# A two-layer decoder trunk in split float32: row sums sent behind the blocks' reads, squares added before their sums, one weight chunk in other buffers

## The chip, the cores and the metric

The kernel runs on one core of a Trainium2 chip. The metric is device time in microseconds of one execution, median of the runs. PE is TensorE (matmuls; PEld its weight loads), DVE is VectorE, ACT ScalarE, POOL GpSimd, SP SyncE, which here issues nearly all DMAs. Each engine works through its own queue in order and waits for the others on semaphores.

## What is computed

512 tokens and 16 meta tokens (T = 528) of width 1024 pass two layers. Each layer is an RMS norm, one wide input projection, two parallel mixers (causal pooling in four groups, and latent attention with 8 heads), gates, an up-projection each and an output projection on the residual:

```python
for l in range(DEPTH):
    h = rmsnorm(h_res, norm_gain[l])
    proj = h @ w_in[l]
    u_pool, z_pool, c_q, c_kv, k_rope, z_mla, g_pool, g_mla = jnp.split(proj, IN_SPLIT_POINTS, axis=-1)
    y_pool = (pool_mix(u_pool, pool_w_group[l], pool_scale[l]) * jax.nn.silu(z_pool)) @ pool_w_up[l]
    o_mla = mla(c_q, c_kv, k_rope, pos, q_a_norm_gain[l], kv_a_norm_gain[l], w_q_b[l], w_kv_b[l],
                q_norm_gain[l], k_norm_gain[l])
    y_mla = (o_mla * jax.nn.silu(z_mla)) @ mla_w_up[l]
    merged = jax.nn.sigmoid(g_pool) * y_pool + jax.nn.sigmoid(g_mla) * y_mla
    h_res = h_res + merged @ w_out[l]
```

Inside `mla` the compressed queries (768 wide) and keys (256 wide) are normed, expanded to 8 heads of 64 plain and 32 rotary dimensions, normed again per head over those 96 dimensions (query and key), rotated and used in causal softmax attention. The result is float32.

## The kernel before

**Tiles.** All activations lie transposed: 128 channels on partitions, up to 528 tokens along the free dimension, worked in halves of 264 (`FULL`) or, in the last layer, in one stretch of 512. Every large matmul is done as three (`mm3`, L204 on): weights and activations are each split in a high and a low part, and hi x hi, hi x lo and lo x hi are summed in PSUM (L205 to L207). Weights come in chunks of 128 x 512: `fetch` issues the load into one of three `raw` buffers, ACT makes `whi` (L200), DVE `wlo` (L201). Three buffers each hold these; a chunk marked `spare` goes to a wide buffer (`th`) instead, of which there are two and which the attention also uses.

**Order.** `stream` is one generator of all large matmuls in a fixed order: the compressed keys and queries (ckv, cq), pooling inputs (u), keys (k), values (v), gates of the pool (zp), pooling (y), queries (qr, qn), the up-projection of the pool (pu), the rest of the gates (zm, gp, gm), the attention's up-projection (mu0 to mu7), the output projection (o). `Layer.go` runs the special work and advances the stream between its steps: `up(name)` until a projection is done, `fill_now(ns)` and `fill` for so many planned nanoseconds of matmuls, `after(ns, fn)` puts a function that far on. A scheduler then fixes each engine's order. `behind(a, b)` makes a wait for b, `follow(a, b)` keeps only the order.

**Norm sums.** The squares of the tokens (layer 1: `square_x`, in tiles `cq` and `q`; layer 0 sums the tokens by rows on ACT) and of the two halves of the compressed keys (`csq`, L485) are summed over channels by a matmul with a block of ones (L426): each uses 32 columns, so that four stand side by side in the array, at positions 0, 32, 64 and 96, two token halves times two inputs. POOL adds the token squares in pairs and pairs of pairs first (L382), which leaves two tiles. The rotary key follows at once in matmuls of the same form (`kr_sums`, L501). The sums go to DRAM and back, spread over 16 partitions (`nq`), are turned into inverse roots by DVE in small steps (`newton`), and are read back for all partitions.

**Statistics.** For the norms per head, squares of keys, rotary keys, queries (four tiles qn, 64 plain dimensions of two heads each) and rotary queries (two tiles qr, 32 dimensions of four heads each) are summed by matmuls of 16 columns with blocks of ones as weights (`stat_go`, L535), again at four positions: two token halves, two in turn. `q_stat` makes the squares of the queries on ACT (L730).

**Attention.** For each head `prep` copies the head's keys and queries together (POOL, L807 to L811), `head` computes scores for blocks of 128 queries, their exponentials (ACT, L840, into `pa`, `cq8`, `cq10`) and row sums (`rs`), and transposes the blocks into `attD` (DVE, L846). The blocks go to DRAM (`pdr`, L906) and come back in another order in four reads of `attE` (L915); ACT and DVE split them (`parts`, L958, L959), and `pv` multiplies with the values (L980, L983) two heads later. The row sums go to DRAM (`rdr`, L907) and come back spread over 64 partitions (L920, a `cq` tile); for every second head, POOL multiplies the gate with them (L924). POOL also saves 16 columns of each block (L843) from the buffers of the exponentials. The reads are put `BACK` (7800) planned nanoseconds on, the gate `LATE` (13000).

```python
            via = pdr[h % 2]
            sp.dma_start(via, blocks)
            sp.dma_start(row.rearrange("a (p i) -> p (a i)", i=4), rs[:, 0:4])
```

Of the kernel before, what the change touches and what calls it, by code (L numbers as in the profile page):

```python
# [19 lines left out]
DEPTH = 2  # L20
D = 1024
# [9 lines left out]
NEG = -1e30  # L31
TWO_PI = 2.0 * math.pi
SWAP = [i ^ 16 for i in range(32)]
MAGIC = float(1.5 * 2.0 ** 23)
# [46 lines left out]
def trunk(ctx, tc, xT, xrow, mrow, pos, win, wkr, wqb, wkb, wvb, wgr, wpu, wmu, wout, gains, const, yT):  # L81
# [255 lines left out]
    scr = dp.tile([P, 8, SEQ], F32, name="scr")  # L337
    nsr = [dp.tile([4, T], F32, name=f"nsr{l}") for l in range(DEPTH)]
    ndr = [dp.tile([3, T], F32, name=f"ndr{l}") for l in range(DEPTH)]
# [8 lines left out]
    class Layer:  # L348
        def __init__(self, l):
            self.l, self.last = l, l == DEPTH - 1  # L350
            self.XS = XTOK if self.last else FULL
            self.x0 = NM if self.last else 0
            self.xt = xt if l == 0 else [None] * 8
            self.hs, self.us, self.zps = hbuf, [None] * 4, [None] * 4
            self.cs, self.cqs, self.ys, self.am = [None] * 2, [None] * 6, [None] * 4, [None] * 8
            self.kn, self.qn, self.zms, self.ogs = [None] * 4, [None] * 4, [None] * 4, [None] * 4
            self.qr, self.qf = [None] * 2, [None] * 2
            self.gms, self.mg, self.xr, self.vw = [None] * 8, [None] * 8, [None] * 8, []
            self.made = [None] * 8
            self.csq, self.xsq = [None] * 2, [None] * 8  # L360
            self.sq, self.half = [], halves()
            self.hosted = self.st = self.acc = self.inv = self.cinv = self.kraw = self.kp = None
# [13 lines left out]
        def square_x(self, k):  # L376
            self.xsq[k] = slot(f"cq{4 + k}" if k < 4 else f"q{k}")
            made = act.activation(self.xsq[k][:, :T], self.xt[k][:, :T], AF.Square)
            for w in (1, 2):
                if k % (2 * w) == 2 * w - 1:  # L380
# [26 lines left out]
        def norm_sums(self):  # L407
            if self.l:
                fill_now(2600)
            else:  # L410
# [11 lines left out]
            for k in range(0, len(runs), 2):  # L422
                for s, (a, b) in enumerate(FULL):
                    for ps, t, m, start, stop in runs[k:k + 2]:
                        g = 64 * s + 32 * (m % 2)
                        mm = pe.matmul(ps[g:g + 32, :HALF], ones[:, 0:32], t[:, a:b], start=start, stop=stop,  # L426
                                       tile_position=(0, g))
                        if t is not self.csq[1]:
                            behind(mm, self.csq_last)
            self.kr_sums()  # L430
            sums = tmp()
            for s, (a, b) in enumerate(FULL):
                if self.l:
                    act.activation(sums[0:64, a:b], px[64 * s:64 * s + 64, :HALF], AF.Copy)
                dve.tensor_copy(sums[64:128, a:b], pc[64 * s:64 * s + 64, :HALF])
            raw, norms = nsr[self.l], ndr[self.l]
            if self.l:
                sp.dma_start(raw, sums[0:97:32, 0:T])
            else:
                sp.dma_start(raw[2:4], sums[64:97:32, 0:T])  # L440
# [5 lines left out]
            nq = sm.tile([16, 4, C], F32, tag="nq", name=nm("nq"))  # L446
# [3 lines left out]
            dve.scalar_tensor_tensor(out=na[:, 0, :], in0=nq[:, 1, :], scalar=1.0 / D, in1=na[:, 0, :],  # L450
                                     op0=ALU.mult, op1=ALU.add)
            dve.tensor_scalar(na[:, 1, :], na[:, 0, :], EPS, None, op0=ALU.mult)
            dve.tensor_scalar(ny[:, 2, :], na[:, 1, :], EPS, None, op0=ALU.mult)
            for m in range(2):
                dve.scalar_tensor_tensor(out=na[:, 1, :], in0=nq[:, 2 + m, :], scalar=1.0 / 256,
                                         in1=na[:, 1, :], op0=ALU.mult, op1=ALU.add)
            newton(ny[:, 0:2, :], na, nt)
# [266 lines left out]

        def q_stat(self, ps, a, b, c):
            for a0, b0 in FULL:
                a0, b0 = max(a, a0), min(b, b0)
                if a0 < b0:
                    q = next(self.half)
                    made = act.activation(q[:, :b0 - a0], ps[:, a0 - a:b0 - a], AF.Square)  # L730
                    self.stat(q[:, :b0 - a0], a0, b0, c, made)

        def ev_qr(self, r):
            def ev(ps, a, b):
# [4 lines left out]
                act.activation(f[:, a:b], ps, AF.Copy, scale=self.g(G_QR))  # L739
                self.q_stat(ps, a, b, C_IR + 4 - 4 * r)  # L740

# [4 lines left out]
        def ev_qn(self, p):  # L746
            def ev(ps, a, b):
                if a == self.x0:
                    self.qn[p] = slot(f"q{p}")
                act.activation(self.qn[p][:, a:b], ps, AF.Copy, scale=self.g(G_QN))  # L750
                self.q_stat(ps, a, b, C_IK + 6 - 2 * p)
            return ev

        def qk_stats(self):
            fill_now(LAG + 100)
            self.stat_go()
# [36 lines left out]
        def prep(self, h):  # L793
            p, odd = h // 2, h % 2
            n0, r0 = (64, 0) if odd else (0, 64)
            kd = self.ks[p][odd]
            g0 = 32 * (h % 4)
            qh, ql = qhl[odd]
# [11 lines left out]
            for d, f in zip((qh, ql), self.qr[h // 4]):  # L810
                gp.tensor_copy(d[r0:r0 + 32, x0:T], f[g0:g0 + 32, x0:T])  # L811
            m = P if odd else QK
            return [t[0:m] for t in (*kd, qh, ql)]

        def head(self, h, kq, prev):
# [96 lines left out]
            def back():  # L912
                got.append(att("E"))
                for b in range(4):
                    behind(sp.dma_start(got[0][32 * b:32 * b + 32, :].bitcast(F32).rearrange("k (a x) -> k a x", a=4),  # L915
                                        via[:, n * b:n * b + n].rearrange("(a k) x -> k a x", a=4)), newest[0])
                if odd == 0:
# [9 lines left out]
            if odd == 1:  # L927
                after(LATE, gate)
            return h, got
# [150 lines left out]
        def register(self, nxt):  # L1080
# [146 lines left out]
def constants():  # L1227
# [5 lines left out]
    c[64:128, C_IK + 15] = 1.0  # L1233
    for i in range(4):
        c[32 * i:32 * i + 32, C_IR + 12 + i] = 1.0
    c[0:32, C_KPE:C_KPE + 8] = 1.0
# [12 lines left out]
def arrange(x, positions, meta_tokens, norm_gain, w_in, pool_w_group, pool_scale, pool_w_up, q_a_norm_gain,  # L1249
# [16 lines left out]
    no, ro = np.arange(64), 64 + np.arange(32)  # L1266
    cols = np.concatenate([QK * h + ro for h in range(H)] + [QK * h + no for h in range(H)])
    wqb = tiles(w_q_b[:, :, cols])
# [27 lines left out]
```

## Time and profile before

| What | us |
|---|---|
| Median of 3 runs (756.3 to 756.56) | 756.54 |
| The profiled execution | 756.64 |
| Its span, first to last instruction | 754.9 |
| PE busy | 749.7 |
| DVE busy | 548.1 |
| ACT busy | 395.9 |
| POOL busy | 218.8 |

Layer 0 fills the span to about 390 us, layer 1 the rest; the attention runs from 177 to 309 and from 557 to 680. Rows of groups read: line, engine, operation, output<-inputs, shapes, count, then busy time in all and mean nanoseconds of one, then the idle time of that engine just before them and what ended it. Rows of the timeline and of the chain of waits begin with start and length in us. In the list of waits the columns are total, times and longest. Matmuls overlap in their records, so the distance of their starts tells what one costs.

### The profile page before, as it was taken

The numbers are of one execution on the slowest core, as the hardware profiler recorded it, in microseconds if no ns is written. First come the engines' busy times: TensorE is split into PE (matmuls) and PEld (weight loads), VectorE is DVE, ScalarE is ACT, GpSimd is POOL, SyncE is SP. The second block draws the span as 40 slices with busy tenths as digits, with TensorE's granted clock in tenths as the row PEclk, the third lists the DMA queues.
The fourth block names the chain that finished last, engine by engine and source line by source line (L and its number), as shares of the span: only waits on it lengthen the run. The fifth ranks groups of instructions, "written<-read, shape, count | busy, mean of one in ns | idle before, by whom it ended". The sixth has DMA issues, their size and how long they took to land.

```text
span 754.9 us, 14329 instructions
## 1 busy us (share of the span) xinstructions
PE 749.7 (99%) x5038; PEld 682.9 (90%) x5038; DVE 548.1 (73%) x1209; ACT 395.9 (52%) x866; POOL 218.8 (29%) x267
## 2 busy tenths in 40 slices
PE   9999999999999999999999999999999999999998
PEld 8999899999999999999997898887788888888887
DVE  5588777457999988684466477676478999975942
ACT  6755655645565665542355446456345666653321
POOL 1126404204463620061130264023044435111400
PEclk9999999999999999999999999999999999999999
DMA  8532223443765567525642322234447756773472
GB/s 316 162 108 89 74 82 86 113 116 119 211 186 166 151 194 192 156 86 157 183 145 85 114 84 66 89 90 120 108 135 210 190 156 181 195 200 93 127 227 84
DMA packets 72853, 106.58 MB, mean 141 GB/s; under 512 B 14102, under 2 KB 34966, under 8 KB 72780
## 3 DMA queue, kind: packets, MB, share of 16 engines
q1 hardware_dynamic: 72636, 105.39, 47.6%
q8 instruction: 40, 0.66, 0.4%
q14 instruction: 33, 0.27, 0.1%
q10 hardware_dynamic: 144, 0.26, 0.1%
HBM read 89.76 MB, written 15.86 MB: 140 GB/s over the span
## 4 chain that ended last, share of the span: by engine, by line
PE 98%; DMA 1%; ACT 0%; SPq 0%; issue 0%; DVE 0%; ACTq 0%
PE mm L205 29%; PE mm L207 29%; PE mm L206 29%; PE S L205 2%; PE S L207 2%; PE S L206 2%; PE o L980 1%; PE o L983 1%; PE S L535 1%; PE S L881 1%; DMA attE<-pdr 1%; PE S L501 0%; DMA xb<-xT 0%; PE mm L995 0%; PE mm L426 0%
## 5 line engine op out<-in xcount | busy, mean ns | idle before, releaser
L205 PE MATMUL mm<-hh,whi 128*128 128x264 f32 (+2 forms) x1072 | 336.1, 315 | 0.6 <-ACT whi L200 0.6
L206 PE MATMUL mm<-hl,whi 128*128 128x264 f32 (+2 forms) x1072 | 336.6, 315 | 0.0
L207 PE MATMUL mm<-hh,wlo 128*128 128x264 f32 (+2 forms) x1072 | 336.4, 316 | 0.0
L201 DVE TENSOR_TENSOR wlo<-raw,whi 128x512 fp32r<-128x512 f32 (+2 forms) x238 | 173.4, 730 | 95.8 <-ACT whi L200 92.4
L200 ACT ACTIVATE whi<-raw 128x512 fp32r<-128x512 f32 (+2 forms) x238 | 142.3, 600 | 176.1 <-PE mm L206 136.4
L205 PEld LDWEIGHTS mm<-hh,whi 128*128 128x128 f32 x1072 | 201.3, 188 | 15.0 <-issue 0.8
L206 PEld LDWEIGHTS mm<-hl,whi 128*128 128x128 f32 x1072 | 201.6, 188 | 12.9
L207 PEld LDWEIGHTS mm<-hh,wlo 128*128 128x128 f32 x1072 | 200.9, 188 | 12.3
L649 POOL TENSOR_TENSOR racc<-racc,tmp 128x264 f32<-128x264 f32 (+1 forms) x15 | 14.4, 959 | 132.3 <-ACT tmp L648 132.3
L1055 POOL TENSOR_TENSOR tmp<-tmp,xb 128x264 f32<-128x264 f32 (+1 forms) x24 | 27.0, 1137 | 49.1 <-DVE tmp L1053 46.4
L833 DVE CUSTOM_DVE_ANT_0 S<-S,maskw,nqs 128x240 f32<-128x240 f32 (+4 forms) x80 | 37.8, 492 | 4.2 <-PE S L207 3.9
L811 POOL CAST qhl<-q 32x528 fp32r<-32x528 f32 (+1 forms) x32 | 25.1, 800 | 44.2 <-PE S L881 42.9
L809 POOL CAST kh<-cq 32x528 fp32r<-32x528 f32 x16 | 15.6, 976 | 69.8 <-issue 36.1
L206 PE MATMUL mm<-th,whi 128*128 128x264 f32 (+1 forms) x108 | 34.7, 321 | 0.0
L205 PE MATMUL mm<-cq,whi 128*128 128x264 f32 (+1 forms) x108 | 34.7, 321 | 0.0
L205 PE MATMUL mm<-u,whi 128*128 128x264 f32 (+1 forms) x108 | 34.6, 321 | 0.0
L206 PE MATMUL mm<-cq,whi 128*128 128x264 f32 (+1 forms) x108 | 34.5, 321 | 0.0
L207 PE MATMUL mm<-cq,wlo 128*128 128x264 f32 (+1 forms) x108 | 34.5, 321 | 0.0
L207 PE MATMUL mm<-u,wlo 128*128 128x264 f32 (+1 forms) x108 | 34.5, 319 | 0.0
L959 DVE TENSOR_TENSOR attE<-attE,th 128x640 fp32r<-128x640 f32 x32 | 26.9, 862 | 3.7 <-ACT th L958 3.7
L840 ACT ACTIVATE cq<-S,bia 128x400 f32<-128x400 f32 (+2 forms) x48 | 24.4, 511 | 9.2 <-DVE bia L894 7.7
L843 POOL COPY pm<-cq 128x16 f32<-128x16 f32 x32 | 18.2, 570 | 37.7 <-ACT cq L840 37.5
(301 smaller groups left out, 1369.5 us busy)
## 6 DMA issues: line engine op xcount, KB each, us to landing
raw<-win SPq DMA_DIRECT2D x143, 256.0 KB, 3.2
pdr<-attD SPq DMA_DIRECT2D x16, 640.0 KB, 3.7
attE<-pdr SPq DMA_DIRECT2D x64, 160.0 KB, 3.9
raw<-wout SPq DMA_DIRECT2D x32, 256.0 KB, 2.8
raw<-wpu SPq DMA_DIRECT2D x16, 256.0 KB, 2.7
raw<-wmu SPq DMA_DIRECT2D x16, 256.0 KB, 2.7
raw<-wqb SPq DMA_DIRECT2D x12, 256.0 KB, 2.6
xb<-xT SPq DMA_DIRECT2D x8, 264.0 KB, 5.5
```

What stands on the lines that cost most here:

```text
L200: act.activation(hi[:, :n], raw[:, :n], AF.Copy)
L201: dve.tensor_sub(lo[:, :n], raw[:, :n], hi[:, :n].bitcast(F32))
L205: first = pe.matmul(out, wh, xh, start=start, stop=False)
L206: pe.matmul(out, wh, xl, start=False, stop=False)
L207: newest[0] = pe.matmul(out, wl, xh, start=False, stop=stop)
L809: gp.tensor_copy(d[r0:r0 + 32, :], f[g0:g0 + 32, :])
L811: gp.tensor_copy(d[r0:r0 + 32, x0:T], f[g0:g0 + 32, x0:T])
L833: return dve.tensor_tensor_reduce(out=sv, in0=sv, in1=mask, scale=nqs[:, i, h:h + 1], scalar=3e38, op0=ALU.add, op1=ALU.min, accum_out=bia ...
L840: act.activation(pv, sv, AF.Exp, scale=-1.0, bias=bia[:, i:i + 1], accum_out=rs[:, c:c + 1])
L843: gp.tensor_copy(pm[:, i, 16 * odd:16 * odd + 16], pt[i][:, 0:NM])
L959: dve.tensor_sub(got[:, a:b], f[:, a:b], hi[:, a:b].bitcast(F32))
L1055: gp.tensor_add(t[:, :b - a], t[:, :b - a], self.am[m][:, a:b])
```

## The change

Five edits, none of which changes what is computed:

- **Tokens and compressed keys.** `square_x` adds the token squares down to one tile (one more level, `w` = 4). POOL adds the second half of the compressed keys' squares to the first, and the sums by ones wait for this addition. Of the sums by ones, layer 0 keeps one input (positions 32 and 96), layer 1 two; the DRAM rows and the small DVE steps shrink with them.
- **Queries.** The squares of the rotary queries (`r` given) are kept instead of being summed, and added to those of the plain queries, 32 partitions at a time: POOL for the first three tiles, DVE for the last. So that a head's rotary part lies on partitions where its plain part lies, the heads of a rotary tile change seats (`SEAT`); `prep` and the host's order of the weights follow. The four matmuls of a layer for rotary squares go, and the statistics come 600 planned nanoseconds later.
- **Row sums.** The write to `rdr` moves behind the four reads of `attE`, and its read a further `BACK / 3` on. The last head's gate comes after `BACK` instead of `LATE`.
- **Up-projection.** mu1 is no longer `spare`: its weights go to `whi` and `wlo`.

```diff
@@ square_x
-            for w in (1, 2):
+            for w in (1, 2, 4):
@@ norm_sums
-            px, pc = mmt() if self.l else None, mmt()
-            xs = self.xsq[::4] if self.l else []
-            runs = [(px, t, m, m < 2, m >= len(xs) - 2) for m, t in enumerate(xs)]
-            runs += [(pc, t, m, True, True) for m, t in enumerate(self.csq)]
...
+            ps, c = mmt(), self.csq[0]
+            self.csq_last = gp.tensor_add(c[:, :T], c[:, :T], self.csq[1][:, :T])
+            runs = [(self.xsq[0], 0)] * self.l + [(c, 32)]
+            for i, (a, b) in enumerate(FULL):
+                for t, m in runs:
+                    g = 64 * i + m
+                    mm = pe.matmul(ps[g:g + 32, :HALF], ones[:, 0:32], t[:, a:b], start=True, stop=True,
+                                   tile_position=(0, g))
+                    behind(mm, self.csq_last)
@@ q_stat
-                    q = next(self.half)
-                    made = act.activation(q[:, :b0 - a0], ps[:, a0 - a:b0 - a], AF.Square)
-                    self.stat(q[:, :b0 - a0], a0, b0, c, made)
+                    q, n = next(self.half), b0 - a0
+                    made = act.activation(q[:, :n], ps[:, a0 - a:b0 - a], AF.Square)
+                    if r is not None:
+                        self.rsq[r, a0] = q
+                        continue
+                    eng = dve if p == 3 else gp
+                    for g in (0, 64):
+                        g += 32 * (p % 2)
+                        made = eng.tensor_add(q[g:g + 32, :n], q[g:g + 32, :n], self.rsq[p // 2, a0][g:g + 32, :n])
+                    self.stat(q[:, :n], a0, b0, C_IK + 6 - 2 * p, made)
@@ qk_stats
-            fill_now(LAG + 100)
+            fill_now(LAG + 700)
@@ head
-            sp.dma_start(row.rearrange("a (p i) -> p (a i)", i=4), rs[:, 0:4])
...
+                    read = sp.dma_start(got[0][32 * b:32 * b + 32, :].bitcast(F32).rearrange("k (a x) -> k a x", a=4),
+                                        via[:, n * b:n * b + n].rearrange("(a k) x -> k a x", a=4))
+                    behind(read, newest[0])
+                follow(sp.dma_start(row.rearrange("a (p i) -> p (a i)", i=4), rs[:, 0:4]), read)
+                after(BACK / 3, sums)
+
+            def sums():
...
-                after(LATE, gate)
+                after(LATE if h + 1 < H else BACK, gate)
@@ register
-                plan[-1].spare = m % 2 == 1
+                plan[-1].spare = m % 2 == 1 and m > 1
```

What it does to the order is seen at three places. Line numbers of the change run one to nine off those of before: L205 to L207 are L206 to L208, L426 is L425, L501 is L499, L574 and L576 L572 and L574, L735 is new, L980 and L983 are L989 and L992. The numbers at the names' ends are those of buffers.

First, TensorE at the sums by ones of layer 1. Before (`cq` and `q` with 5133 and 5392 are the token squares, the other two those of the compressed keys):

```order
L206 MATMUL mm_5780<-hl_19_159,whi_5776 128x512
L207 MATMUL mm_5780<-hh_18_158,wlo_5777 128x512
L426 MATMUL mm_5805<-cq_853_5133,ones 32x264
L426 MATMUL mm_5805<-q_892_5392,ones 32x264
L426 MATMUL mm_5805<-cq_853_5133,ones 32x264
L426 MATMUL mm_5805<-q_892_5392,ones 32x264
L426 MATMUL mm_5806<-q_937_5684,ones 32x264
L426 MATMUL mm_5806<-q_948_5755,ones 32x264
L426 MATMUL mm_5806<-q_937_5684,ones 32x264
L426 MATMUL mm_5806<-q_948_5755,ones 32x264
L501 MATMUL S_5816<-xb,kn_926_5629 32x264 x8
```

With the change:

```order
L207 MATMUL mm_5792<-hl_19_159,whi_5788 128x512
L208 MATMUL mm_5792<-hh_18_158,wlo_5789 128x512
L425 MATMUL mm_5817<-cq_854_5144,ones 32x264
L425 MATMUL mm_5817<-q_938_5696,ones 32x264
L425 MATMUL mm_5817<-cq_854_5144,ones 32x264
L425 MATMUL mm_5817<-q_938_5696,ones 32x264
L499 MATMUL S_5824<-xb,kn_927_5641 32x264 x8
```

Four matmuls are left, one at each position.

Second, POOL ahead of the statistics of layer 0, where it finishes the rotary queries (`q`). Before, the copies of head 0 follow:

```order
L576 TENSOR_TENSOR q_331_1889<-q_331_1889,tmp_1892 128x264
L576 TENSOR_TENSOR q_331_1889<-q_331_1889,tmp_1907 128x264
L809 COPY kh_2459<-cq_419_2453 32x528
L807 COPY kh_2459<-kh_2457 64x528
L809 COPY kl_2460<-cq_420_2454 32x528
```

With the change:

```order
L735 TENSOR_TENSOR attD_1958<-attD_1958,xb 32x264 x4
L574 TENSOR_TENSOR q_331_1887<-q_331_1887,tmp_1890 128x264
L735 TENSOR_TENSOR attD_1958<-attD_1958,xb 32x264 x2
L574 TENSOR_TENSOR q_331_1887<-q_331_1887,tmp_1905 128x264
L735 TENSOR_TENSOR attD_1958<-attD_1958,xb 32x264 x2
L735 TENSOR_TENSOR attE_2077<-attE_2077,xb 32x264 x4
L814 COPY kh_2476<-cq_419_2470 32x528
```

Twelve additions stand among and behind the last two rotary steps (the squares lie in `attD`, `attE` and `xb` at that time). DVE has four more of them, with one weight subtraction between the second and the third.

Third, TensorE at the product with V of head 5, whose end frees the `attE` buffer of head 6's reads. Before:

```order
L980 MATMUL o_4247<-th_4134,vt 128x512
L205 MATMUL mm_4154<-hh_16_156,whi_4149 128x264
L206 MATMUL mm_4154<-hl_17_157,whi_4149 128x264
L983 MATMUL o_4247<-attE_3953,vt 64x512
L980 MATMUL o_4247<-th_4134,vt 128x384
```

With the change:

```order
L989 MATMUL o_4264<-th_4151,vt 128x512
L992 MATMUL o_4264<-attE_3968,vt 64x512
L989 MATMUL o_4264<-th_4151,vt 128x384
L992 MATMUL o_4264<-attE_3968,vt 64x384
L989 MATMUL o_4264<-th_4151,vt 128x256
```

The two large matmuls inside the product have moved behind it. From its last matmul to the first of head 6's product stand 57 large and small matmuls before, and 60 with the change.

More of the change, by code (lines that the diff above doesn't have):

```diff
@@ L337, in trunk @@
     scr = dp.tile([P, 8, SEQ], F32, name="scr")
-    nsr = [dp.tile([4, T], F32, name=f"nsr{l}") for l in range(DEPTH)]
+    nsr = [dp.tile([3 - l, T], F32, name=f"nsr{l}") for l in range(DEPTH)]
     ndr = [dp.tile([3, T], F32, name=f"ndr{l}") for l in range(DEPTH)]
@@ L445, in norm_sums @@
             fill_now(2600)
-            nq = sm.tile([16, 4, C], F32, tag="nq", name=nm("nq"))
+            nx = 2 - self.l
+            nq = sm.tile([16, nx + 1, C], F32, tag="nq", name=nm("nq"))
             na, nt, ny = (sm.tile([16, n, C], F32, tag=t, name=nm(t)) for t, n in (("na2", 2), ("nt2", 2), ("ny2", 3)))
@@ L1266, in arrange @@
     no, ro = np.arange(64), 64 + np.arange(32)
-    cols = np.concatenate([QK * h + ro for h in range(H)] + [QK * h + no for h in range(H)])
+    cols = np.concatenate([QK * (h - h % 4 + SEAT[h % 4]) + ro for h in range(H)] + [QK * h + no for h in range(H)])
     wqb = tiles(w_q_b[:, :, cols])
```

44 lines of the change are left out of this document (16 added, 28 removed).

## The prediction

> **What bounds the kernel now.** I read the page first: is one engine busy all the time?
>
> ```profile
> span 754.9 us, 14329 instructions
> PE 749.7 (99%) x5038; PEld 682.9 (90%) x5038; DVE 548.1 (73%) x1209; ACT 395.9 (52%) x866; POOL 218.8 (29%) x267
> PEclk9999999999999999999999999999999999999999
> PE 98%; DMA 1%; ACT 0%; SPq 0%; issue 0%; DVE 0%; ACTq 0%
> ```
>
> TensorE works through 99% of the span at full clock and holds 98% of the chain of waits. Next, who it ever waited for:
>
> ```profile
> PE wps L157 <- DVE na L764: 1.1, 1, 1.1
> PE mm L205 <- ACT whi L200: 0.6, 1, 0.6
> PE S L205 <- ACT hh L371: 0.2, 1, 0.2
> ```
>
> That is the whole list: 1.9 us, of which 1.3 lie at the start. So time goes down only by taking work off TensorE, and goes up by whatever makes it wait. The chain of waits shows the pieces that the change touches (start, us, engine and line):
>
> ```profile
> 24.81 0.58 PE mm L426 x8
> 25.39 1.78 PE S L501 x32
> ...
> 149.32 2.80 PE S L535 x48
> ...
> 285.25 4.36 DMA attE<-pdr
> ...
> 290.35 0.73 ACT th L958
> 291.13 0.50 PE o L980
> ...
> 319.65 0.25 PE mm L206 x2
> ...
> 405.28 1.03 PE mm L426 x16
> ...
> 528.08 2.80 PE S L535 x46
> ...
> 671.31 0.47 PE mm L207 x2
> ```
>
> The sums by ones and the statistics (L426, L501, L535) are float32 matmuls with 16 or 32 columns of weights, at four column positions; each leaves two records (a few are missing in the x46). Of the big matmuls, two of 264 columns take 0.25 and two of 512 take 0.47. How long does one take? The timeline of TensorE inside the statistics:
>
> ```profile
> 151.05 0.63 PE L535 MATMUL S<-attD,cst 128*16 128x264 f32 x8
> 151.50 0.63 PE L535 MATMUL S<-attE,cst 128*16 128x264 f32 x8
> ```
>
> Eight records, four matmuls at four positions, take 151.50 - 151.05 = 0.45 us; it is the round of four that costs 0.45, not the single matmul. The 48 records of L535 are six rounds: 6 x 0.45 = 2.7, and the chain says 2.80.
>
> **What the change removes.** In layer 1 the sums by ones go from eight matmuls to four, two rounds to one: -0.45. The statistics lose the four matmuls of the rotary query squares, 24 to 20, six rounds to five: -0.45 in each layer. In layer 0 the sums go from four matmuls to two, at positions 32 and 96. The matmuls of L501 behind them need the same positions: before, (8 + 32) records / 4 positions = 10 passes on each; now positions 32 and 96 still have 2 + 8 = 10. So I take 0; the bounds are 0 and one half round, -0.22. Sum of the removed work: -1.35 us.
>
> **What it adds and moves.** Each added operation stands on POOL or DVE ahead of a matmul that waits for it.
>
> Squares of tokens and of the compressed keys. One more 128x528 addition ends the tree (layer 1), and one adds the two key squares (both layers):
>
> ```profile
> L382 POOL TENSOR_TENSOR q<-q,q 128x528 f32<-128x528 f32 x3 | 4.8, 1584 | 9.1 <-ACT q L378 9.1
> ...
> 21.72 0.66 ACT L485 ACTIVATE q<-mm 128x264 f32<-128x264 f32 x2
> 401.48 0.39 ACT L485 ACTIVATE q<-mm 128x264 f32<-128x264 f32 x1 [0.79 <-DVE kl L483]
> ```
>
> The last squares end at 22.4 and 401.9; with 1.58 behind them the sums are there at 24.0 and 403.5, and TensorE comes at 24.8 and 405.3. The token tree would end before that too (its last addition of before ends at 391.92 + 3.51 in the row quoted further down, 395.4, plus 1.58 = 397.0, with the key sum behind it). Cost 0; without that cover 1.6 each.
>
> Squares of queries. In each layer 12 additions of 32 partitions go to POOL and 4 to DVE; the statistics begin 600 ns of planned matmuls later, and the order has nine more big matmuls of 264 columns ahead of them in layer 0 (9 x 0.125 = 1.1 us) and five of 512 in layer 1 (5 x 0.235 = 1.2). The trace has no such addition; the nearest rows bound one on POOL (the first two are groups, count | busy, mean ns; the others timeline rows of POOL and ACT):
>
> ```profile
> L515 POOL COPY kp<-kp 32x264 f32<-32x264 f32 x12 | 6.2, 520 | 8.1 <-DVE kp L513 7.6
> L576 POOL TENSOR_TENSOR kp<-kn,tmp 128x264 f32<-128x264 f32 x4 | 4.3, 1087 | 1.5 <-DVE tmp L574 1.3
> ...
> 132.36 2.06 POOL L575 TENSOR_TENSOR q<-q,tcos 128x264 f32<-128x264 f32 x2
> 134.38 1.93 POOL L576 TENSOR_TENSOR q<-q,tmp 128x264 f32<-128x264 f32 x2
> ...
> 391.92 3.51 POOL L382 TENSOR_TENSOR q<-q,q 128x528 f32<-128x528 f32 x2
> ...
> 514.34 1.71 POOL L811 CAST qhl<-q 32x512 fp32r<-32x512 f32 x2
> ...
> 146.43 0.40 ACT L730 ACTIVATE attE<-mm 128x264 f32<-128x264 f32 x1
> ...
> 522.76 0.65 ACT L730 ACTIVATE attE<-mm 128x248 f32<-128x248 f32 x2
> ```
>
> Between 0.52 (a 32-partition copy) and 1.09 (a two-input operation on 128 partitions); I take 0.8, nearer the two-input row. In layer 0 POOL is free of L575 at 134.4; 12 x 0.8 and the two L576 of 0.97 end at 145.9, at 1.09 each at 149.4. Layer 1: free at 516.05, done at 525.7, at most 529.1. DVE's last two additions follow the last squares (146.8, 523.4), with one L201 between at most; at L201's mean of 0.73 (its row stands below) for each, they end at 149.0 and 525.6. The statistics begin at 149.3 + 1.1 = 150.4 in layer 0 and, with 0.9 already saved, at 528.1 + 1.2 - 0.9 = 528.4 in layer 1. Cover 4.5 and 2.7 us at my value, 1.0 and -0.7 at the upper bound. Cost 0.
>
> One page speaks against this: the Trainium skill, "SBUF — State Buffer", section "Who interferes with whom", says that a VectorE instruction with two SBUF inputs and a GpSimd instruction that reads SBUF exclude each other for a whole instruction. Here the subtraction of L201 runs 0.73 us on average, and one that met POOL's copies took 1.10, which fits:
>
> ```profile
> L201 DVE TENSOR_TENSOR wlo<-raw,whi 128x512 fp32r<-128x512 f32 (+2 forms) x238 | 173.4, 730 | 95.8 <-ACT whi L200 92.4
> 173.55 0.99 POOL L807 CAST kh<-kh 64x528 fp32r<-64x528 f32 x1
> 173.97 1.10 DVE L201 TENSOR_TENSOR wlo<-raw,whi 128x512 fp32r<-128x512 f32 x1
> ```
>
> Row sums behind the blocks' reads. The small write (rs to rdr) moves from ahead of the four reads of attE to behind them, and the read that spreads it over partitions waits for its landing. TensorE never waits for these, but POOL's gate (L924) does, and POOL works in order:
>
> ```profile
> 204.47 2.50 SPq L915 DMA_DIRECT2D attE<-pdr  x4
> 207.07 0.45 SPq L920 DMA_DIRECT2D cq<-rdr  x1
> ...
> DMA to landing us min/median/max: 2.6/3.6/4.1
> ...
> 210.89 2.30 POOL L924 TENSOR_TENSOR u<-u,cq 128x512 f32<-128x512 f32 x1 [1.14 <-DMA cq<-rdr]
> ...
> 219.38 0.47 ACT L840 ACTIVATE pa<-S,bia 128x272 f32<-128x272 f32 x1
> ```
>
> For head 1: the write is issued at 207.0, lands 3.6 later (row of the rdr tile) at 210.6, the read then takes 210.89 - 207.07 = 3.8, so the gate starts at 214.4 instead of 210.9 and ends at 216.0 to 216.7. Behind it on POOL stand two small copies that free the buffers of head 2's exponentials; the next writer of pa comes at 219.4, or, since it now stands first of head 3's two, some 1.5 us sooner. Cover 1 us or a little less; ACT's own weights (L200) lie chunks ahead of TensorE. Cost 0, and the price without cover is rival C.
>
> The other side of this edit, and of the order around it: head 6's first product with V came 0.2 us late, after the reads (285.25 + 4.36), ACT's copies (290.35 + 0.73) and a start at 291.13. The chain starts when the product before it lets go of its attE buffer. In the order, two big matmuls that stood inside head 5's product now stand behind it, and one more has come into the gap: three in all, 3 x 0.125 = 0.37 us more room. I take the whole 0.2 as gone; bounds 0 and -0.2.
>
> The chunk mu1 in the ordinary weight buffers rather than the wide ones: no wait of TensorE stands near mu in either layer, so 0; if its weights came late, one subtraction of L201, 0.73 us. In layer 0 one tiny addition leaves DVE's queue ahead of the only wait in mid-kernel (0.6 us, whi L200, near 57 us):
>
> ```profile
> 40.17 0.17 DVE L455 SCALAR_TENSOR_TENSOR na<-nq,na 16x33 f32<-16x33 f32 x1
> ```
>
> I take -0.1, between 0 and -0.6.
>
> Sum: -1.35 - 0.2 - 0.1 = -1.65. The profiled execution took 756.64 (span 754.9, 1.7 around it), the median is 756.54, 0.1 less; the span goes to 753.25, the median to 754.9.
>
> **The rivals.** A is the forecast, 754.9, with its own range 754.4 to 755.4. B: POOL's additions outlast their cover, by the bound of 1.09 each and a subtraction of 0.7 on DVE now and then in the way (by the page's lock it would be so). Layer 1 is then 0.7 late, layer 0 about 0.5: 756.1. For it: that upper bound; against: DVE's wait list shows slack and the copies of 32 partitions at 0.52. C, the other sign: the gates. If the spread read takes the 4.7 median that its issue row shows, or the write 4.1, each gate slips a further 1.4 us, POOL's casts of the next keys and queries (L809, L811) move with it, and the scores come late:
>
> ```profile
> cq<-rdr SPq DMA_DIRECT2D x16, 128.0 KB, 4.7
> ```
>
> It decides from a slip of about 1 us beyond my reckoning on; 0.6 us on TensorE at each of six gates (the last of a layer has no scores behind it) is +3.6: 758.5. Against it: casts for the next head follow the gate only many microseconds later. D: besides A, the wait of 0.6 at whi goes too, since DVE is rid of an operation and its small ones are spread otherwise: 754.4. E: the change doesn't do what it says: the round isn't what costs, and the passes left run longer; only the 0.3 of the two waits is gained: 756.2.
>
> **Chances.** A 0.58, D 0.12, B 0.12, E 0.05, C 0.13. About 0.2% (1.5 us, below 755.03) is what a measurement of this kernel can tell from no change. A lies just under it, so I give 0.38 of its 0.58 to faster, with D 0.50; the rest of A, B and E make 0.37 for the same; C 0.13 for slower. The range takes in D, A, B and E: 753.9 to 756.5; outside it C and a little at the low end.
>
> **What would show it.** Right: L535 with 40 records in each layer and about 2.35 us, the sums by ones of layer 1 with 8 records and about 0.55, no wait in front of either, TensorE's busy time down by about 1.3, and no entry for POOL among its waits. Wrong: a wait of TensorE for the additions (B), for POOL casts or DVE behind a gate (C), or statistics that take 2.8 still (E). If the big matmuls' spacing of 0.12 changed, none of these cases would be right.

## The result: 0.14% slower, and the profile after

| | before | with the change |
|---|---|---|
| Median of 22 runs each, us | 756.53 (755.51 to 757.26) | 757.26 (756.12 to 759.20) |
| Ratio to before, 95% interval | | 1.0014 (1.0008 to 1.0020) |
| The profiled execution, us | 756.64 | 757.15 |
| Its span | 754.9 | 755.4 |

The forecast was 754.9. Not only the median moved: the runs now spread over 3.1 us, before over 1.8. The head of the page, with the shares of the chain of waits:

```profile
span 755.4 us, 14311 instructions
PE 749.2 (99%) x5010; PEld 682.1 (90%) x5010; DVE 561.2 (74%) x1214; ACT 394.9 (52%) x864; POOL 240.9 (32%) x294
PE 93%; DVE 4%; DMA 2%; issue 1%; ACT 0%; SPq 0%; DVEq 0%; ACTq 0%
```

TensorE is busy 0.5 us less, where 1.3 was forecast (this sum is a blunt measure: with the same matmuls it is 748.1 in the trace of e13 below and 749.6 in that of e6), DVE 13 and POOL 22 us more, and the chain, 98% TensorE before, now runs over DVE and transfers for 6% of the span. Whom TensorE waited for:

```profile
PE S L989 <- ACT th L967: 1.3, 1, 1.3
PE wps L158 <- DVE na L769: 1.1, 1, 1.1
PE mm L206 <- ACT whi L201: 0.4, 1, 0.4
```

The first row is new; it is the product of head 7 with V in layer 1. The chain of waits has what answers to the rows shown of before, and where the time went:

```profile
149.89 2.36 PE S L533 x40
...
404.36 0.58 PE mm L425 x8
...
527.84 2.35 PE S L533 x38
...
666.40 3.45 DMA pdr<-attD
...
671.23 4.46 DMA attE<-pdr
...
676.44 0.73 ACT th L967
677.21 0.51 PE S L989
...
709.49 1.57 issue
711.06 0.69 DVE hl L305
711.79 0.50 PE mm L207
```

The rounds went as forecast: 2.80 to 2.36, 1.03 to 0.58, 2.80 to 2.35, in sum -1.34. The end of layer 1's statistics, 528.08 + 2.80 = 530.88 before and 527.84 + 2.35 = 530.19 with the change, came 0.69 us earlier, with five more large matmuls of 0.235 already done: TensorE was 1.9 us ahead in all. Then it lost 1.5 at 675.5 (677.21 less the 675.7 at which the matmul before let it start), 0.19 + 0.37 + 0.11 around 711, and smaller bits: 0.5 behind at the end.

At the first loss, ACT's timeline before (the last three exponentials of head 7, then the split of head 6's blocks):

```profile
659.30 0.46 ACT L840 ACTIVATE cq<-S,bia 128x240 f32<-128x240 f32 x1 [0.19 <-DVE bia L894]
...
660.22 0.38 ACT L840 ACTIVATE pa<-S,bia 128x144 f32<-128x144 f32 x1
...
663.90 1.37 ACT L958 ACTIVATE th<-attE 128x640 fp32r<-128x640 f32 x2 [3.21 <-DMA attE<-pdr]
```

and with the change:

```profile
662.55 1.37 ACT L967 ACTIVATE th<-attE 128x640 fp32r<-128x640 f32 x2 [3.29 <-PE mm L208]
...
664.34 0.44 ACT L845 ACTIVATE cq<-S,bia 128x240 f32<-128x240 f32 x1
...
665.26 0.37 ACT L845 ACTIVATE pa<-S,bia 128x144 f32<-128x144 f32 x1
```

The split has come to stand ahead of the exponentials. It has to wait for head 6's reads and, through `behind`, for a large matmul of TensorE; in this execution that matmul ended last (the row names PE L208). Head 7's blocks leave at 666.40 instead of 662.63.

### The profile page after: what moved, and what is told of

The parts are those of the page before. It is cut to its first block, busy times and chain, and to the rows that moved or that the text cites. A ratio compares the mean times of both kernels' runs of the same rounds, so it can differ in the third digit from the quotient of the medians.

```text
span 755.4 us, 14311 instructions
## 1 busy us (share of the span) xinstructions
PE 749.2 (99%) x5010; PEld 682.1 (90%) x5010; DVE 561.2 (74%) x1214; ACT 394.9 (52%) x864; POOL 240.9 (32%) x294
## 4 chain that ended last, share of the span: by engine, by line
PE 93%; DVE 4%; DMA 2%; issue 1%; ACT 0%; SPq 0%; DVEq 0%; ACTq 0%
PE mm L206 27%; PE mm L208 27%; PE mm L207 27%; PE S L206 2%; PE S L207 2%; PE S L208 2%; DMA pdr<-attD 1%; PE o L989 1%; DVE wlo L202 1%; PE o L992 1%; DVE hl L305 1%; PE S L886 1%; PE S L533 1%; DMA attE<-pdr 1%; PE wps L158 1%
## 5 line engine op out<-in xcount | busy, mean ns | idle before, releaser
L208 PE MATMUL mm<-hh,wlo 128*128 128x264 f32 (+2 forms) x1072 | 337.0, 316 | 0.0
L207 PE MATMUL mm<-hl,whi 128*128 128x264 f32 (+2 forms) x1072 | 336.6, 315 | 0.1
L206 PE MATMUL mm<-hh,whi 128*128 128x264 f32 (+2 forms) x1072 | 335.9, 315 | 0.4 <-ACT whi L201 0.4
L202 DVE TENSOR_TENSOR wlo<-raw,whi 128x512 fp32r<-128x512 f32 (+2 forms) x240 | 179.2, 750 | 85.3 <-ACT whi L201 82.5
L206 PEld LDWEIGHTS mm<-hh,whi 128*128 128x128 f32 x1072 | 201.3, 188 | 15.1 <-DVE vt L699 0.8
L207 PEld LDWEIGHTS mm<-hl,whi 128*128 128x128 f32 x1072 | 201.6, 188 | 13.1 <-DVE hl L305 0.4
L208 PEld LDWEIGHTS mm<-hh,wlo 128*128 128x128 f32 x1072 | 201.0, 188 | 12.4 <-DVE wlo L202 0.5
L816 POOL CAST qhl<-q 32x528 fp32r<-32x528 f32 (+1 forms) x32 | 27.9, 886 | 40.7 <-PE S L886 39.5
L206 PE MATMUL mm<-cq,whi 128*128 128x264 f32 (+1 forms) x108 | 34.7, 321 | 0.0
L207 PE MATMUL mm<-th,whi 128*128 128x264 f32 (+1 forms) x108 | 34.6, 321 | 0.0
L208 PE MATMUL mm<-u,wlo 128*128 128x264 f32 (+1 forms) x108 | 34.5, 320 | 0.0
L207 PE MATMUL mm<-cq,whi 128*128 128x264 f32 (+1 forms) x108 | 34.5, 321 | 0.0
L208 PE MATMUL mm<-cq,wlo 128*128 128x264 f32 (+1 forms) x108 | 34.5, 321 | 0.0
L206 PE MATMUL mm<-u,whi 128*128 128x264 f32 (+1 forms) x108 | 34.4, 319 | 0.0
L933 POOL TENSOR_TENSOR u<-u,cq 128x512 f32<-128x512 f32 x8 | 13.9, 1739 | 63.5 <-DMA cq<-rdr 46.6
L967 ACT ACTIVATE th<-attE 128x640 fp32r<-128x640 f32 x32 | 21.8, 727 | 13.4 <-DMA attE<-pdr 5.7
```

What stands on the lines that cost most here:

```text
L202: dve.tensor_sub(lo[:, :n], raw[:, :n], hi[:, :n].bitcast(F32))
L206: first = pe.matmul(out, wh, xh, start=start, stop=False)
L207: pe.matmul(out, wh, xl, start=False, stop=False)
L208: newest[0] = pe.matmul(out, wl, xh, start=False, stop=stop)
L816: gp.tensor_copy(d[r0:r0 + 32, x0:T], f[gq:gq + 32, x0:T])
L967: behind(act.activation(hi[:, a:b], f[:, a:b], AF.Copy), newest[0])
```

## The experiments

Ratios are to the kernel before, run beside it on the same chip (its median differs from chip to chip, 755.4 to 756.5, so that ratios of different groups of runs are compared with care). A trace is one execution, and can differ from its median: those of e1 (756.01) and e4 (758.47) are the shortest of their runs. Single traces also differ where no edit has touched anything yet: in e9 and e14 every engine has the order of before up to the statistics of layer 0, and yet TensorE starts these at 148.05 and 148.79, against 149.32 before.

**First group: is it the order at head 7, the later statistics, or mu1?** Theory Q blamed the order just shown. In the first run, e1, that order alone is put back on the changed kernel (`self.ex` is head 7's last exponential):

```diff
@@ parts
-                behind(act.activation(hi[:, a:b], f[:, a:b], AF.Copy), newest[0])
+                made = act.activation(hi[:, a:b], f[:, a:b], AF.Copy)
+                behind(made, newest[0])
+                if self.last and h == H - 2:
+                    follow(made, self.ex)
```

> The changed kernel, with one order fixed: in layer 1 ACT takes the last three exponentials of head 7 ahead of the split of head 6's blocks (th from attE); no work is added or taken away. Theory Q (queue order): the 1.5 us that TensorE waits at head 7's product with V comes from these exponentials standing behind a split that waits for its reads until 662.5; put first they end some 3 us earlier, head 7's blocks leave that much sooner, and the wait of 1.3 to 1.5 goes: 757.26 - 1.5 = 755.8 (755.4 to 756.2). Rival M (memory): the blocks' write and reads are simply slower (3.45 and 4.46 us in this trace), the order does not matter, the wait stays above 1 us: 757.0 to 757.5.

Measured 757.52, ratio 1.0025 (1.0015 to 1.0035): nothing was won. Its waits and chain:

```profile
PE S L992 <- ACT th L967: 1.0, 1, 1.0
```

```profile
663.14 4.50 DMA pdr<-attD
...
670.02 3.58 DMA attE<-pdr
673.71 1.38 ACT th L967 x2
```

The blocks did leave 3.3 us earlier, but the write took 4.50, another DMA got between the reads, the scheduler put the product four big matmuls earlier, and TensorE still waited. Q as the whole story falls. The other three runs:

```diff
@@ the change, later statistics undone (e2)
-            fill_now(LAG + 700)
+            fill_now(LAG + 100)
@@ the change, mu1 spare again (e3)
-                plan[-1].spare = m % 2 == 1 and m > 1
+                plan[-1].spare = m % 2 == 1
@@ before, later statistics alone (e4)
-            fill_now(LAG + 100)
+            fill_now(LAG + 700)
```

> The changed kernel with the statistics at their old place (600 planned ns earlier); all other edits stay. Theory Q: the old order of ACT at head 7 of layer 1 comes back with it, so the wait of 1.5 there goes; the statistics start some 1.1 us earlier, while POOL's last addition ended 2.9 (layer 0) and 1.4 us (layer 1) ahead of them and DVE's 0.9 and 2.0 us, so a wait of 0 to 0.3 each appears; the head 6 wait of 0.2 in layer 0 may come back: 755.6 to 756.4. Rival B (additions): without the 600 ns the additions end after TensorE has come, each layer waits 0.5 to 1 us there, and it is no faster than the change: 757 or more. Rival M: 757.2, with the wait at head 7 still there.

Measured 754.77, ratio 0.9992 (0.9983 to 1.0000). The sign turns with this one number, and TensorE waited for no addition. Rival M falls too: head 7's reads take 4.5 us to land in this trace, 4.0 to 4.5 in that of the change, and TensorE does not wait for them in layer 1. (The profiled execution, at 756.31 the longest of its 11, waits 1.1 at head 7 of layer 0.)

> The changed kernel with chunk mu1 of the up-projection in the wide buffer again. Theory Q: the wait at head 7 stays at 1.3 to 1.5; of the two gaps of TensorE near 711 in layer 1's output projection (0.19 + 0.37, behind DVE's low parts hl) those due to the order of weight splits go: 756.6 to 756.9. Rival (mu1 has no part in it, DVE is simply full there): 757.0 to 757.4, the gaps stay. Rival M2 (mu1's buffers delay head 7 through the wide buffers): the wait at head 7 goes, 755.8.

Measured 757.57, ratio 1.0024 (1.0015 to 1.0034). The two gaps near 711 are gone from the trace; a wait of 1.7 at head 7 and one of 0.8 for `racc` more than make up for them.

> The kernel before with the statistics 600 planned ns later and nothing else: no matmul is removed, no addition made, no write moved. Theory Q: this alone turns the order of ACT at head 7 of layer 1; TensorE waits about 1.5 us there, the 0.2 at head 6 of layer 0 goes: 756.5 + 1.3 = 757.8 (757.3 to 758.2). Rivals B and C (the additions or the moved row sums cost the time): as before, 756.3 to 756.6, no new wait.

Measured 761.11, ratio 1.0072 (1.0058 to 1.0086): with no matmul removed, no addition and no write moved, the 600 planned ns cost more than the whole change does. Waits and chain of this run:

```profile
PE S L980 <- ACT th L958: 2.3, 1, 2.3
...
PE S L983 <- DVE attE L959: 0.8, 1, 0.8
```

```profile
653.05 4.27 DMA pdr<-attD
...
658.70 4.16 DMA attE<-pdr
662.96 0.75 ACT th L958
...
665.89 0.56 DVE attD L846
666.81 3.52 DMA pdr<-attD
...
671.69 4.99 DMA attE<-pdr
676.78 0.74 ACT th L958
677.55 2.60 DVE attE L959 x2
```

Two heads' round trips through DRAM stand end to end: head 6's write, its reads, its split, then head 7's transposes, write, reads, split. That is four transfers of 3.5 to 5.0 us in a row, whose lengths change from execution to execution.

Counted in TensorE's order, the statistics of e4 stand behind as many big matmuls as before; what 600 ns move are the heads. In layer 1 the scores of heads 0 to 5 come 2 to 6 big matmuls later (head 5 behind 3904 instead of 3899), while the scores of heads 6 and 7 and the products from head 4 on come 1 to 3 earlier, since the layer's matmuls end there: the last heads are pressed together. (Where the expectations from here on place heads' scores, they number the heads one too high: head 6 there is head 5. Head 7's product is head 7's.) Alone, the shift costs more than within the change (0.22% between the change and e2, which ran in different groups): here the last gate still meets DVE's split of head 7 (2.60 us, 1.56 in the change) and the clock falls (last section). How much each of these costs was not tried.

**Second group: theory S, the shift.** The next stretch of matmuls gives the 600 ns back (e5), mu1 is undone besides the later statistics (e6), the query squares come alone (e7), and the shift is made three times as large on the kernel before (e8, `LAG + 1900`).

```diff
@@ go, the change (e5)
             kq = self.prep(0)
-            fill_now(2600)
+            fill_now(2000)
```

> The changed kernel with the second of the two stretches of planned matmuls between the statistics and the first head cut from 2600 to 2000 ns, which gives back the 600 that the statistics took; all edits stay. Theory S (shift): what costs is that the heads stand 4 to 5 big matmuls later in TensorE's order while the end of the layer's weights does not move, so that the chain of four transfers from head 5's reads to head 7's product with V in layer 1 has no slack left; here head 6's scores stand 11 big matmuls earlier than in the change (2.6 us), the wait of 1 to 2 us at head 7 goes, and the time is 0.4 to 1.2 us under the kernel before. Rival Q (only the order of ACT at head 7, which here still has head 6's split ahead of the last exponentials): the wait stays, 1 to 2 us over before.

Measured 755.83, ratio 0.9990 (0.9982 to 0.9999), with head 6's split still ahead of the exponentials, and in its trace no wait at head 7 of layer 1: head 5's scores stand 11 big matmuls earlier than in the change, head 7's 3 earlier and its product 4 later. S stands, Q does not.

> The changed kernel with both the later statistics and mu1's buffers undone: sums, query squares and row sums stay. Theory S: as with the later statistics undone alone (0.6 us under before), and TensorE's two gaps of 0.56 in sum in layer 1's output projection, which came with mu1's place in the order of weight splits, go too: 0.9 to 1.4 us under before. Rival: mu1 has no part in these gaps (DVE is full there), and the time is 0.4 to 0.7 under before, gaps still there.

Measured 756.63, ratio 0.9998 (0.9988 to 1.0008). The gaps at 711 went, but waits of 0.3 to 0.4 stand at 259, 261 and 689 us in its trace (757.33); one of 0.6 at 58 is in the trace of before as well.

> The kernel before with the query squares added ahead of their sums and nothing else; the statistics keep their old planned place. The two rounds of statistics go (-0.9). Theory S: the heads stay at their places, no wait at head 7: 0.5 to 1.0 us under before. Rival B (the additions cost by themselves, through the statistics or through DVE and POOL running into each other): TensorE waits ahead of the statistics, or in front of weights, 0 to 1 us over before.

Measured 756.35, ratio 1.0002 (0.9993 to 1.0010): no wait for the additions, and no gain either.

> The kernel before with the statistics planned 1800 ns later in place of 600, nothing else: head 6's scores stand 15 big matmuls later than before in TensorE's order, where 600 ns put them 5 later. Theory S: the wait at the end of layer 1 grows with the shift, to 4 us or more, and where it passes some 3 us the granted clock falls for a while after it (the runs with 600 ns had mean clocks of 0.996 to 0.999): 6 to 12 us over before. Rival Q: the order on ACT at head 7 is another one again (two of the three exponentials' neighbours have changed places), so the wait does not grow with the shift: 0 to 4 us over before.

Measured 763.52, ratio 1.0101 (1.0081 to 1.0120): the loss grows with the shift, though the wait at head 7 is 3.2 us where 4 or more was expected (head 5's scores stand 15 big matmuls later).

**Third group: the other edits alone, and both losses taken away.** Three runs have one edit of the change on the kernel before; e12 is e5 with mu1 spare again.

> The kernel before with chunk mu1 in the ordinary weight buffers and nothing else. Theory S: the other order of the weight splits in layer 1's output projection puts DVE's low parts hl behind TensorE there, the two gaps of 0.19 and 0.37 near 711 come with it: 0.3 to 0.7 us over before. Rival (my prediction): nothing waits at mu, 0 within 0.2; or the gaps come only when TensorE is earlier than before, then 0 as well.

Measured 757.02, ratio 1.0009 (1.0001 to 1.0018). The gaps near 711 are there without any of the other edits (TensorE's timeline; 0.23 is the usual distance):

```profile
709.79 0.39 PE L206 MATMUL mm<-hl,whi 128*128 128x512 f32 x1
710.21 0.50 PE L207 MATMUL mm<-hh,wlo 128*128 128x512 f32 x1
710.81 0.50 PE L206 MATMUL mm<-hl,whi 128*128 128x512 f32 x1
```

They stand in all five traces with mu1 in ordinary buffers (the change, e1, e2, e5, e9) and in none of the others.

> The kernel before with only the sums by ones cut (tokens to one tile, compressed keys added on POOL). One round of matmuls in layer 1 goes (-0.45) and one tiny DVE step. Theory S: nothing later is moved in the planned order, so most of it shows: 0.2 to 0.7 us under before, no wait in front of the sums. Rival (every gain is lost again at head 7's product, whose chain of transfers does not get shorter): 0 within 0.2.

Measured 755.95, ratio 0.9999 (0.9991 to 1.0008). In its trace (756.87, above its median) head 7's low part came 0.7 us late: DVE's split of the blocks and POOL's last gate fell together. They do so in the trace of before too, where the two operations of the split take 2.92 us and TensorE still comes 0.9 us after their end. DVE's timeline of e10 and POOL's:

```profile
676.23 2.78 DVE L956 TENSOR_TENSOR attE<-attE,th 128x640 fp32r<-128x640 f32 x2 [3.02 <-ACT th L955]
```

```profile
676.03 1.55 POOL L921 TENSOR_TENSOR u<-u,cq 128x512 f32<-128x512 f32 x1 [15.80 <-DMA cq<-rdr]
```

> The kernel before with only the row sums' write behind the reads and the last gate earlier planned. No matmul goes. Theory S: 0 within 0.3; the last gate on POOL (L924, 2.12 us in the trace of before) no longer meets DVE's split of head 7's blocks, whose two operations take 1.6 together in place of 2.9. Rival C (gates slip, casts and scores behind them come late): 1 us or more over before, with a wait of TensorE behind POOL or DVE in the heads.

Measured 756.39, ratio 1.0004 (0.9995 to 1.0013). The gates cost nothing that can be told; rival C of the prediction falls.

> The changed kernel with the 600 planned ns given back ahead of the first head and mu1 in the wide buffer again: both losses that the traces show are taken away and all removed matmuls stay removed. Theory S: 0.9 to 1.5 us under before (1.35 of rounds; small waits of 0.2 to 0.4 at the products of head 7). Rival (the gain is lost at other places as soon as TensorE is earlier, as when the later statistics and mu1 were both undone): 0 to 0.6 under before.

Measured 755.63, ratio 0.9996 (0.9987 to 1.0004), its profiled execution 754.86. With both losses out, 1.35 us of rounds still do not show in the median: the interval reaches 1.0 us under before.

**Fourth and fifth group: why does the removed work not show?** Theory E: the end of layer 1 eats it. So the heads get room there, with the removed rounds (e13: e6 with `fill_now(2000)`) and on the kernel before (e14).

> The changed kernel with the later statistics and mu1's buffers undone, and the stretch ahead of the first head 600 planned ns shorter: in layer 1 head 6's scores stand 6 and head 7's 11 to 15 big matmuls earlier than in the kernel before (1.4 to 3.5 us), its product with V 3 later. Theory E (the end of layer 1 eats the gain): with this room no wait at head 7's product, and the removed rounds show: 0.9 to 1.6 us under before. Rival W (waits spread over the kernel, wherever TensorE comes earlier): 0 to 0.5 under before, as with the later statistics and mu1 undone.

> The kernel before with only the stretch ahead of the first head 600 planned ns shorter: the same room at the end of layer 1, no round removed. Theory E: the kernel before has 0.9 to 2 us of slack at head 7's product in its trace, so there is little to win: 0 to 0.4 us under before. Rival W: 0 within 0.2, or slower where the earlier heads meet other work.

Measured 756.05, ratio 1.0002 (0.9993 to 1.0010), and 756.29, ratio 0.9998 (0.9989 to 1.0007). As the whole story theory E falls as well: no wait is left at head 7 of layer 1, and e13 waits elsewhere, all in layer 0 (the first and the third around head 7 there; the second, near 57 us, is in the trace of before too):

```profile
PE mm L1004 <- DVE cq L1053: 0.6, 1, 0.6
PE mm L206 <- ACT whi L201: 0.5, 1, 0.5
PE S L989 <- ACT th L967: 0.3, 1, 0.3
```

Then the round itself: dropped, doubled, and the additions made with no round saved. The orders of the other engines do not change by it.

```diff
@@ q_stat, before (e15; e16 makes it twice instead)
-                    self.stat(q[:, :b0 - a0], a0, b0, c, made)
+                    if c < C_IR:
+                        self.stat(q[:, :b0 - a0], a0, b0, c, made)
@@ q_stat, query squares alone (e17)
                         self.rsq[r, a0] = q
+                        self.stat(q[:, :n], a0, b0, C_IR + 4 - 4 * r, made)
```

> The kernel before with the four matmuls of a layer for the squares of the rotary queries left out and nothing put in their place (the norms of the queries then miss their rotary part); the order of all other engines is word for word the same. Theory P (a round off TensorE is worth its 0.45 us, and what took back the gain of the query squares are the additions): 0.7 to 1.0 us under before. Theory W (TensorE's lead is lost in waits for others): 0 to 0.4 under before.

> The kernel before with these four matmuls of a layer made twice (the rotary part then counts double in the queries' norms), nothing else: one round more in each layer. Theory P: 0.7 to 1.0 us over before. Theory W: the waits shrink as TensorE comes later: 0 to 0.5 over before.

> The kernel with the query squares alone (labelled so above), with the four matmuls of a layer put back against columns of zeros: the additions are made, no round is saved. Theory P: the additions cost what the rounds saved, 0.6 to 1.1 us over before. Theory W: as TensorE's lead counts little, 0 to 0.5 over before, about as much as the query squares alone plus nothing.

Measured 755.88, ratio 0.9999 (0.9991 to 1.0008); 756.86, ratio 1.0012 (1.0003 to 1.0021); 756.22, ratio 1.0003 (0.9994 to 1.0012). A round more in each layer costs about its 0.9 us; a round less, with nothing put in its place, gives 0.1 by the ratio, at best 0.7; the additions alone cost 0.2. The doubled round fits theory P, the other two theory W, though P's 0.7 lies on the edge of e15's interval; neither holds all three.

One pattern the traces do show. In e7, e10 and e15, which remove rounds and leave the last gate where it was, TensorE waits at the same place, head 7's product in layer 1, for DVE's low part (one row from each list of waits):

```profile
PE S L991 <- DVE attE L967: 0.6, 1, 0.6
PE S L980 <- DVE attE L956: 0.7, 1, 0.7
PE S L984 <- DVE attE L960: 0.6, 1, 0.6
```

In all three the split meets POOL's last gate and takes 2.78 to 2.82 us. That is not all of it: e6 removes the same rounds, its gate is moved, its split takes no part in a wait, and it gains nothing either.

## Why the prediction was wrong

**What held.** A round of four costs 0.45 us (2.80 to 2.36 for six to five), the two matmuls less in layer 0 nothing. (No records are missing in the x46, as I had read it: the trace of before has 96 of L535, 48 a layer.) The additions of 32 partitions took 0.89 us on POOL where I took 0.8 (its additions and multiplications of 128x264 took 0.79 to 1.09 a group before, so fewer partitions saved little or nothing), and their cover held without the 600 ns too (e2). The group's row and POOL's last additions in the changed kernel, ahead of statistics at 527.84:

```profile
L735 POOL TENSOR_TENSOR attD<-attD,xb 32x264 f32<-32x264 f32 x12 | 10.9, 906 | 0.8
```

```profile
514.76 8.15 POOL L735 TENSOR_TENSOR attD<-attD,xb 32x248 f32<-32x248 f32 x8
522.99 3.44 POOL L735 TENSOR_TENSOR attE<-attE,xb 32x248 f32<-32x248 f32 x4
```

Head 1's gate started at 214.56, forecast 214.4. Head 6's wait in layer 0 went, but the -0.2 set down for it was no gain of the change: the traces of e9, e11 and e14, with the order of before at that product, do not have the wait either. The -0.1 for the wait near 57 us can't be told: that wait is 0.4 in the change's trace, 0.2 to 0.7 or absent in the others. Rivals B, C, D and E did not come to pass; C had the sign, not the mechanism.

**The step that failed** is the one on the query squares: "the statistics begin 600 ns of planned matmuls later ... Cost 0". I asked what is hidden ahead of the statistics, not what is planned behind them. The statistics were moved by the additions (they stand as late in e2 and e7, without the 600 ns), not by the 600 ns; these moved the heads, and the cost put at nothing is, in the trace of the change, the 1.5 us at head 7's product. The kernel before had little to give there: the split of head 7's blocks ended 2 us (the high part, on ACT) and 0.9 us (the low part, on DVE) ahead of its product. The runs put the step at +0.72% alone (e4), and its removal from the change turns 0.14% slower into 0.08% faster (e2), its compensation into 0.10% faster (e5); these ratios come from different chips.

**The second**: "no wait of TensorE stands near mu in either layer, so 0". Alone, mu1 costs 0.09% (0.01 to 0.18). Undone in the change and its variants it brought nothing that can be told (e3 1.0024, e6 0.9998, e12 0.9996), so its share of the loss is less sure than the gaps. Its place shifts the weight splits of the output projection, and on DVE's timeline of the change one of them stands in front of the low part that TensorE needs at 711. It takes 1.78 us, the mean of its group being 0.77, and a multiplication of POOL runs beside it (third row):

```profile
709.35 1.78 DVE L202 TENSOR_TENSOR wlo<-raw,whi 128x512 fp32r<-128x512 f32 x1
711.06 0.68 DVE L305 TENSOR_TENSOR hl<-tmp,hh 128x512 fp32r<-128x512 f32 x1
...
708.97 1.61 POOL L1064 TENSOR_TENSOR tmp<-tmp,xb 128x512 f32<-128x512 f32 x1 [1.29 <-DVE tmp L1062]
```

A wait that is absent before says nothing on how near it is.

**The third** is the conclusion drawn at the start, "time goes down only by taking work off TensorE": true, but the reverse was taken with it, that each us taken off is a us of time. e7, e10 and e15 take off 0.9, 0.45 and 0.9 and give nothing that can be told; in their traces waits of 0.6 to 0.7 stand at head 7's product, in those of e6, e12 and e13 waits of 0.3 to 0.6 elsewhere. That these are the same us is not shown for the medians; which engine sets the pace then stays open.

The smallest time against before is the change with the 600 ns given back (e5); e2 lies beside it.

## What to carry to other kernels

Before a step in a planned order is put later, find what is planned behind it and where that ends: if the end is fixed, the step's delay comes out of the slack of the last round trip, however well the step itself is covered. With TensorE at 99%, added work cost about its price here (e16), but removed work gave nothing that can be told (e15): see how far ahead of it the others finish (0.9 and 2 us at the last product here), not only whether it waits. Where the chain of transfers lost its slack, the runs also spread wider: 3.1 us with the change, 1.8 before.

## What the runs showed of the hardware

**A long wait costs twice.** In e8 TensorE stood still from 679.9 to 683.04. Stretches of the trace (length, then TensorE's, weight loads', DVE's, ACT's and POOL's busy time, granted clock, DMA):

```profile
679.00:683.00 4.00, 0.86 (x4) 0.38 (x2) 0.60 (x1) 1.36 (x2) 0.85 (x1) 1.00 1.06 246
683.00:686.00 3.00, 2.96 (x7) 2.27 (x8) 3.00 (x4) 2.26 (x4) 0.68 (x1) 0.52 0.06 16
686.00:689.00 3.00, 3.00 (x16) 2.46 (x16) 2.28 (x5) 1.23 (x2) 0.00 (x0) 0.91 0.56 165
```

```profile
684.03 0.63 PE L207 MATMUL mm<-hh,wlo 128*128 128x512 f32 x1
684.46 0.63 PE L205 MATMUL mm<-hh,whi 128*128 128x512 f32 x1
```

Behind the wait the granted clock is 0.52 over 3 us and 0.91 over the next 3, and matmuls start every 0.43 us instead of 0.23: 3 x 0.48 + 3 x 0.09 = 1.7 us more. In e4's trace a wait of 2.3 left the clock at 1.00, but of its six runs five had a mean clock of 0.996 to 0.998, by estimate 1.5 to 3 us of lost clock in 760; of the change's 22 runs the two longest, 759.08 and 759.20, had 0.998, by the same estimate 1.5 us. Where in these runs the clock was low no trace shows. The Trainium skill, "TensorE: Matmul & The Clock Gate", section "What's actually happening", gives half the clock after about one idle window of 3.4 us and a busy one to come back; this trace about agrees: the wait was 3.2 us, a little under a window, and the 1.7 us lost are those of 3.4 us at half the clock.

**DVE and POOL.** The same two operations of DVE took 2.78 us beside a POOL multiplication in e10 (above), and 1.56 in e2, where the gate started only at 678.23:

```profile
674.47 1.56 DVE L968 TENSOR_TENSOR attE<-attE,th 128x640 fp32r<-128x640 f32 x2 [2.65 <-ACT th L967]
```

That is the exclusion of the Trainium skill, "SBUF — State Buffer", section "Who interferes with whom", which I had weighed for the additions only, where it did not decide.
